# A two-layer hybrid trunk on one core: wide products in the first layer, c broadcast by DMA, and tokens sorted by t mod 4

## The chip, the core and the metric

The kernel runs on one core of a Trainium2 chip. The time is that of the device, in microseconds, for one execution of the whole program; lower is better. Several executions were timed, and one more was recorded by the hardware profiler. In the profile PE is TensorE's matmul, PEld its weight load, DVE is VectorE, ACT ScalarE, POOL GpSimd, and SP the engine whose queue issues all DMAs of this kernel.

## What is computed

One sequence of 256 tokens with 2048 features goes through two layers. Each layer is x <- LayerNorm(alpha x + (1 + gate) mixer(x (1 + scale) + shift)), where shift, scale and gate are products of silu(c) with a 2048 x 6144 matrix ("ada"), c being one vector of 2048.

- Layer A (a state-space mixer): `proj = h @ in_w`, with 4096 columns z, 4096 columns xs, 2048 columns B and C, 64 columns dt. xs, B and C go through a causal convolution of width 4 along the tokens and a silu; then a scan in one chunk of 256 tokens for 8 groups of 8 heads, a gate silu(z), an RMS norm by group, and the product with out_w (4096 x 2048).
- From the output of layer A keys and values are made for 3 groups of 8 heads of 128 (`x @ kv_w`, 2048 x 6144).
- Layer B (attention): 24 query heads in three groups (window, dilation) = (128, 1), (512, 4), (2048, 16). A query t attends t, t - d, t - 2d, ... within its window, with a linear bias in the distance. The outputs of the three groups are merged per head by their softmax denominators, which is one softmax over the keys of all three groups. Then a gate silu(z), and the product with out_w.

With 256 tokens a query of group 2 or 3 can only meet keys of the same t mod 4.

## The kernel before

Everything is in fp32 accuracy. The large products split each weight piece and each activation into a high part in the format fp32r and the low rest, and add three products: high x high, high x low, low x high. A weight piece is 128 x 1024 (512 KB), loaded by `load_piece` (L88) into one of 6 buffers, split by `split` into `whi` by ACT (L94) and `wlo` by DVE (L95), each with 4 buffers. The small products (scores, values, transposes) are in plain fp32.

There are three forms of large product:

- `tm_piece`/`tm_mults` (L172 to L174): the activations are the stationary side, the weights stream with 512 columns.
- `cm_piece` (L119 to L121), run by `cm_quad`, `cm_quads` or by hand: the weights are stationary, 256 tokens stream. For each of the 2 row tiles and 4 column blocks of a piece three matmuls of 256 columns: high x high, high x low, low x high, all into the same 128 x 256 accumulator.
- `cm_wide` (L151, L152): the high and the low half of the activations lie side by side, so one matmul with 512 columns makes high x high and high x low into the two halves of an accumulator of 128 x 512, and one of 256 adds low x high into the first half. A piece has 4 row tiles and 2 column blocks, and the two matmuls follow each other for each of them. At the end the two halves are joined: ACT copies one (L156), DVE adds the other (L157).

The order of the work:

1. *Start.* c is loaded as two rows, spread over the partitions by 8 records of matmul with a column of ones (L422), and silu'd by ACT into `cb_` (L423). Then the 32 tiles of layer A's shift and scale (1 MB each, `ada_load` L230) are multiplied with `cb_` and summed by DVE (`ada_dot` L236), and each finished pair gives one tile of h (`h_step`, L381 to L383), high and low part in `hp`. While these come in, parts of ten products are begun with the tiles of h that are there (`begun`, `order`); each part is set aside in SBUF and later added.
2. *Layer A's products* (`product`), with the scan (`stage1`, `stage2`, `stage3`) of a group beside the products of the next one. `xs` and `bc` products use `cm_quad`; the convolution `conv` reads the accumulator where it is (L302, L305), or the sum with the set-aside part (L344). The dots for the gate run in the background, one in five pieces.
3. *Layer A's output* (L172 to L174 with `ylo`); `y_tiles` (L641 to L644) transposes y two tiles of 128 at a time between the pieces.
4. *LayerNorm, keys and values.* `x_tiles` (L711 to L716) transposes the normalized rows and makes high and low part; three key products by `cm_quads`, three by `cm_wide` (`wk1`), six value products. Beside them 32 more ada tiles. GpSimd multiplies the rows by the LayerNorm's gain and adds its offset (L766, L767) for the residual of layer B.
5. *Layer B*: `queries` by `cm_wide`, `attend` for 4 heads at a time, `z_gate` by `cm_wide`, then the output product and the last LayerNorm.

The order on every engine is not that of the code: `arrange` simulates the whole program with prices for each instruction, gives each a due time, tries several rounds of list scheduling, and fixes the best order per engine, the DMA queue on SP included.

## Time and profile before

| | |
|---|---|
| runs | 1283.16, 1287.76, 1289.54 us; median 1287.76 |
| profiled execution | 1281.55 us, of which the span from first to last instruction is 1279.8 |
| granted TensorE clock | 0.993 |
| DMA | 334.82 MB, mean 262 GB/s |
| busy: PE, DVE, ACT, POOL | 1239.4, 1039.2, 696.6, 33.3 us |

The profiled execution is 1.6 us below the fastest of the three runs and 6.2 below their median. Rows of the profile read: line of the kernel, engine, operation, output<-inputs with shapes, count | busy time, mean ns of one | idle time of the engine just before, and what ended it. A timeline row is start, length, engine, line, operation, names, shapes, count of records merged. A record of a matmul lasts longer than the distance to the next one, since matmuls are pipelined.

### The profile page before, as it was taken

How to read it: one execution, taken by the hardware profiler on the slowest of the kernel's cores; microseconds unless marked ns; L12 is line 12 of the kernel's file. 1: busy time of each engine (PE TensorE's matmuls, PEld its weight loads, DVE VectorE, ACT ScalarE, POOL GpSimd, SP SyncE). 2: the span in 40 equal slices, each digit the busy share in tenths (PEclk: the TensorE clock that was granted, in tenths of full speed). 3: DMA queues.
4: the chain of work that ended last, by engine and by line, in shares of the span. 5: the costliest groups of instructions: out<-in, count | busy, mean ns of one | idle time of the engine just before them, and what ended most of it. 6: DMA issues, size and time to landing. Idle time of an engine off the chain costs nothing.

```text
span 1279.8 us, 19378 instructions
## 1 busy us (share of the span) xinstructions
PE 1239.4 (97%) x7386; PEld 1095.2 (86%) x7386; DVE 1039.2 (81%) x1457; ACT 696.6 (54%) x1027; POOL 33.3 (3%) x20
## 2 busy tenths in 40 slices
PE   6999999999999999999999899999999999999995
PEld 4978999899899999788888699888888888888884
DVE  6999978999998887978895799998745647848778
ACT  4644566868577767764333444444445645444551
POOL 0000000000000000000000135000000000000000
PEclk9999999999999999999999899999999999999998
DMA  9999967887785556578997688999866663453571
GB/s 372 422 422 422 384 216 268 314 276 247 240 300 191 173 159 203 162 258 269 400 376 218 222 315 308 396 420 395 299 191 193 211 185 115 147 183 107 155 266 66
DMA packets 80449, 334.82 MB, mean 262 GB/s; under 512 B 9090, under 2 KB 9314, under 8 KB 67684
## 3 DMA queue, kind: packets, MB, share of 16 engines
q1 hardware_dynamic: 80356, 333.58, 73.5%
q8 instruction: 58, 0.95, 0.3%
q14 instruction: 35, 0.29, 0.1%
HBM read 331.37 MB, written 2.18 MB: 261 GB/s over the span
## 4 chain that ended last, share of the span: by engine, by line
PE 78%; DMA 12%; DVE 7%; ACT 1%; issue 1%; SPq 0%; DVEq 0%; ACTq 0%
PE acc L151 12%; PE acc L174 11%; PE acc L173 11%; PE acc L172 11%; PE acc L152 6%; DMA raw<-in_win 6%; PE acc L119 6%; PE acc L121 6%; PE acc L120 6%; DMA araw<-in_ada 5%; DVE wlo L95 2%; PE py L589 1%; DVE araw L236 1%; PE aux L795 1%; PE po L819 1%
## 5 line engine op out<-in xcount | busy, mean ns | idle before, releaser
L95 DVE TENSOR_TENSOR wlo<-raw,whi 128x1024 fp32r<-128x1024 f32 x395 | 488.9, 1244 | 176.5 <-ACT whi L94 175.2
L94 ACT ACTIVATE whi<-raw 128x1024 fp32r<-128x1024 f32 x395 | 417.1, 1057 | 382.1 <-PE acc L174 178.6
L119 PE MATMUL acc<-actT,whi 128*128 128x256 f32 x960 | 273.6, 288 | 11.8 <-ACT actT L382 7.4
L173 PE MATMUL acc<-wlo,actT 128*128 128x512 f32 x704 | 276.4, 393 | 0.6 <-DVE wlo L95 0.6
L172 PE MATMUL acc<-whi,actT 128*128 128x512 f32 x704 | 274.8, 393 | 1.6 <-ACT whi L94 1.0
L121 PE MATMUL acc<-actT,wlo 128*128 128x256 f32 x960 | 270.5, 285 | 1.4 <-DVE wlo L95 1.4
L120 PE MATMUL acc<-actT,whi 128*128 128x256 f32 x960 | 271.3, 285 | 0.0
L151 PE MATMUL acc<-actT,whi 128*128 128x512 f32 x704 | 251.3, 398 | 0.0
L236 DVE SCALAR_TENSOR_TENSOR araw<-araw,cb__72 128x2048 f32<-128x2048 f32 x96 | 218.4, 2286 | 9.0 <-DMA araw<-in_ada 5.7
L152 PE MATMUL acc<-actT,wlo 128*128 128x256 f32 x704 | 201.8, 287 | 0.6 <-DVE wlo L95 0.6
L119 PEld LDWEIGHTS acc<-actT,whi 128*128 128x128 f32 x960 | 185.2, 194 | 15.7 <-ACT actT L382 9.0
L121 PEld LDWEIGHTS acc<-actT,wlo 128*128 128x128 f32 x960 | 184.0, 193 | 2.3 <-DVE wlo L95 2.0
L120 PEld LDWEIGHTS acc<-actT,whi 128*128 128x128 f32 x960 | 185.1, 193 | 0.3
L174 PE MATMUL acc<-whi,actT 128*128 128x512 f32 x448 | 175.1, 391 | 0.0
L172 PEld LDWEIGHTS acc<-whi,actT 128*128 128x128 f32 x704 | 131.9, 188 | 30.1 <-ACT whi L94 2.8
L151 PEld LDWEIGHTS acc<-actT,whi 128*128 128x128 f32 x704 | 132.2, 188 | 29.2
L173 PEld LDWEIGHTS acc<-wlo,actT 128*128 128x128 f32 x704 | 132.3, 188 | 27.5 <-DVE wlo L95 1.1
L152 PEld LDWEIGHTS acc<-actT,wlo 128*128 128x128 f32 x704 | 133.0, 189 | 1.9 <-DVE wlo L95 1.2
L174 PE MATMUL acc<-whi,ylo 128*128 128x512 f32 x256 | 100.8, 394 | 0.0
L174 PEld LDWEIGHTS acc<-whi,actT 128*128 128x128 f32 x448 | 84.1, 188 | 17.5 <-issue 0.5
L174 PEld LDWEIGHTS acc<-whi,ylo 128*128 128x128 f32 x256 | 48.1, 188 | 9.4
L305 DVE SCALAR_TENSOR_TENSOR cacc<-acc,prm,cacc 128x255 f32<-128x255 f32 (+2 forms) x96 | 43.7, 475 | 2.7 <-ACT cacc L302 2.3
(205 smaller groups left out, 1083.1 us busy)
## 6 DMA issues: line engine op xcount, KB each, us to landing
araw<-in_ada SPq DMA_DIRECT2D x96, 1024.0 KB, 7.2
raw<-in_win SPq DMA_DIRECT2D x160, 512.0 KB, 4.9
raw<-in_wkv SPq DMA_DIRECT2D x72, 512.0 KB, 4.9
raw<-in_wout SPq DMA_DIRECT2D x64, 512.0 KB, 5.6
raw<-in_wbin SPq DMA_DIRECT2D x64, 512.0 KB, 4.0
raw<-in_wk SPq DMA_DIRECT2D x24, 512.0 KB, 6.6
cbc<-cumd SPq DMA_DIRECT2D x16, 512.0 KB, 5.3
raw<-in_wbout SPq DMA_DIRECT2D x16, 512.0 KB, 4.3
```

What stands on the lines that cost most here:

```text
L94: S.activation(hi, raw, AF.Copy)
L95: V.tensor_tensor(lo, raw, hi.bitcast(F32), op=ALU.subtract)
L119: T.matmul(o, hi[:, k, c_], ahi[:, kt, :], start=first, stop=False, skip_group_check=True)
L120: T.matmul(o, hi[:, k, c_], alo[:, kt, :], start=False, stop=False, skip_group_check=True)
L121: T.matmul(o, lo[:, k, c_], ahi[:, kt, :], start=False, stop=kt == k1 - 1, skip_group_check=True)
L151: T.matmul(ps[n], hi[:, k, c_], xp[:, kt], start=kt == 0, stop=False, skip_group_check=True)
L152: T.matmul(ps[n][:, 0, :], lo[:, k, c_], xhi[:, kt, :], start=False, stop=kt == KT - 1, skip_group_check=True)
L172: T.matmul(ps[b], h_, hi[:, k, :], start=kt == k0, stop=False)
L173: T.matmul(ps[b], h_, lo[:, k, :], start=False, stop=False)
L174: T.matmul(ps[b], l_, hi[:, k, :], start=False, stop=kt == k1 - 1)
L236: V.scalar_tensor_tensor(raw, raw, 1.0, cb_, op0=ALU.mult, op1=ALU.mult, accum_out=mod[layer][:, ct, j:j + 1])
L305: V.scalar_tensor_tensor(acc[:, o:], ps[:, :L - o], w[:, j:j + 1], acc[:, o:], op0=ALU.mult, op1=ALU.add)
```

## The change

Nine edits are made together.

- `cm_wide` becomes general and takes over the `xs` and `bc` products 1 to 7 and 2, 4, 6 of layer A (`cm_quad` goes). Their weights come as a new array `wsub` in pieces of 4 row tiles x 256 columns. `hp` is laid out tile by tile with the high and low half side by side. Without a set-aside part the two halves are joined by an ACT copy and a DVE add into a new tile `ct`; with one, DVE adds both halves to it, one after the other.
- In every `cm_wide` the 8 matmuls of 512 columns of a piece come first, then the 8 of 256 columns.
- c is broadcast to all partitions by four DMAs of 512 columns, and silu'd in place; the rows and the 8 matmul records go.
- The first shift and scale tile are loaded and dotted in two halves, whose sums are added.
- `y_tiles` makes the four transposes of two tiles before their reads.
- `x_tiles` writes the tokens sorted by t mod 4, so keys, values, queries and the attention's output are in that order; the gated output is put back in order when it is split, by 8 instructions instead of 2 on each of ACT and DVE.
- In `attend` a block of 128 queries (two classes of t mod 4) takes 128 keys each for the two dilated groups, and 256 for the first: 512 scores in one PSUM tile, where it was 384 for the first block and 768 for the second. The bias of a head is made in 3 instructions, once for both blocks.
- The LayerNorm's gain and offset for the residual go from GpSimd to DVE. The bias table (768 columns of distance and 768 of mask) lies in `cb_` instead of a buffer of its own.
- The planner prices a DMA that writes to DRAM 3 us longer. The order of all engines is planned anew.

```diff
-    def cm_quad(src, ahi, alo, rate=(0, 1), k0=0):
+    def cm_wide(src, both, high, rate=(0, 1), k0=0):
         ps = acc_pair()
-        for q in range(k0 // 2, KT // 2):
-            cm_piece(src, q, ps, ahi, alo, k0=k0)
+        for q in range(k0 // 4, KT // 4):
+            hi, lo = (t.rearrange("p k n -> p (k n)").rearrange("p (k n) -> p k n", k=4)
+                      for t in split(load_piece(src[q])))
+            halves = [(k, n, slice(n * P, n * P + P)) for k in range(4) for n in range(2)]
+            for k, n, c_ in halves:
+                T.matmul(ps[n], hi[:, k, c_], both[:, 4 * q + k], start=4 * q + k == k0, stop=False, skip_group_check=True)
+            for k, n, c_ in halves:
+                T.matmul(ps[n][:, 0, :], lo[:, k, c_], high[:, 4 * q + k, :], start=False, stop=4 * q + k == KT - 1,
+                         skip_group_check=True)
             background(*rate)
         return ps
...
+        n = 2 if (layer, ct) == (0, 0) and kind != "gate" else 1
+        for i in range(n):
+            c_ = slice(D // n * i, D // n * i + D // n)
+            nc.sync.dma_start(raw[:, c_], ada[layer, KIND.index(kind), ct][:, c_])
...
-                ps = cm_quad(src, hhi, hlo, rate=R, k0=k0)
-                t = tiles(ps)
-                if part is not None:
-                    for w in range(2):
-                        V.tensor_tensor(part[:, 2 * w:2 * w + 2, :], ps[w], part[:, 2 * w:2 * w + 2, :], op=ALU.add)
-                    t = [part[:, n, :] for n in range(4)]
+                t = []
+                for w in range(2):
+                    ps = cm_wide(wsub[2 * WSUB.index((kind, g)) + w], hp, hhi, rate=R, k0=k0)
+                    for n in range(2):
+                        if part is None:
+                            t.append(p0.tile([P, L], F32, name="ct", bufs=4))
+                            S.activation(t[-1], ps[n][:, 1, :], AF.Copy)
+                            V.tensor_tensor(t[-1], ps[n][:, 0, :], t[-1], op=ALU.add)
+                        else:
+                            t.append(part[:, 2 * w + n, :])
+                            for i in range(2):
+                                V.tensor_tensor(t[-1], ps[n][:, i, :], t[-1], op=ALU.add)
...
-                for i in range(2):
-                    row = szt[i].rearrange("p b n -> p (b n)")[:1]
-                    nc.sync.dma_start(row, c[:, 1024 * i:1024 * i + 1024])
+                for i in range(4):
+                    bcast(cb_[:, 512 * i:512 * i + 512], c, 512 * i)
+                    S.activation(cb_[:, 512 * i:512 * i + 512], cb_[:, 512 * i:512 * i + 512], AF.Silu)
...
+            pt = pt.rearrange("p (j r) -> p r j", r=4)
-            S.activation(xhi[:, kt, :], pt, AF.Identity, bias=b_, scale=g_)
+            S.activation(xhi[:, kt, :].rearrange("p (r j) -> p r j", r=4), pt, AF.Identity, bias=b_, scale=g_)
...
-                PO.tensor_tensor(u[b][:, cs_], u[b][:, cs_], lnr[0], op=ALU.mult)
-                PO.tensor_tensor(u[b][:, cs_], u[b][:, cs_], lnr[1], op=ALU.add)
+                V.tensor_tensor(u[b][:, cs_], u[b][:, cs_], lnr[0], op=ALU.mult)
+                V.tensor_tensor(u[b][:, cs_], u[b][:, cs_], lnr[1], op=ALU.add)
...
+                for g in (1, 2):
+                    T.matmul(pq[:, (g - 1) * P:g * P], qq[:, g, i, cb], kk[hq][:, g, i, cb], start=True, stop=True)
+                T.matmul(pq[:, 2 * P:], qq[:, 0, i, cb], kk[hq][:, 0, i, :], start=True, stop=True)
...
+            T.matmul(po, v[:, 0, 0, ci], pT[:, :, 2, :], start=True, stop=False)
+            T.matmul(po, v[:, 0, 1, ci], pT[:, :, 3, :], start=False, stop=False)
+            for b in range(2):
+                for g in (1, 2):
+                    T.matmul(po[:, b * P:b * P + P], v[:, g, b, ci], pT[:, b, g - 1, :], start=False, stop=b == 1 and g == 2)
...
-        return 0.36, 0.0, None, _n(o) * list(o.ap)[0][1] * 4
+        return 0.36, 3.0 if str(o.bass_ap.tensor.space) == "DRAM" else 0.0, None, _n(o) * list(o.ap)[0][1] * 4
```

More of the change, by code (lines that the diff above doesn't have):

```diff
@@ L266, in drain @@
             jobs.pop(0)()
[L269 to L270 removed]
+    hp = act.tile([P, KT, 2, L], F32R, name="actT")
+    hhi, hlo = hp[:, :, 0, :], hp[:, :, 1, :]
     with ExitStack() as cA:
@@ L419, in trunk @@
                 nc.sync.dma_start(adab_, par[:, :NB])
-                for i in range(4):
-                    pc = mm.tile([P, 512], F32, name="acc")
-                    T.matmul(pc, ones[:1, :], szt[i // 2][:1, i % 2, :], start=True, stop=True)
-                    S.activation(cb_[:, 512 * i:512 * i + 512], pc, AF.Silu)
                 V.tensor_scalar(adab[:, :, :, 1:3], adab[:, :, :, 1:3], 1.0, None, op0=ALU.add)
```

134 lines of the change are left out of this document (64 added, 70 removed).

## The prediction

> **What bounds the kernel now.** I read the page from the top: the busy shares, the 40 slices, the chain. Then I cut the span into stages with the view of windows, because the shares are means over stages with different limits.
>
> ```profile
> span 1279.8 us, 19378 instructions
> PE 1239.4 (97%) x7386; PEld 1095.2 (86%) x7386; DVE 1039.2 (81%) x1457; ACT 696.6 (54%) x1027; POOL 33.3 (3%) x20
> PE 78%; DMA 12%; DVE 7%; ACT 1%; issue 1%; SPq 0%; DVEq 0%; ACTq 0%
> ```
> ```profile
> 17.00:132.00 115.00, 108.77 (x667) 96.74 (x668) 106.19 (x114) 60.39 (x81) 0.00 (x0) 1.00 1.02 422
> 150.00:540.00 390.00, 388.15 (x2695) 359.25 (x2693) 343.15 (x541) 278.57 (x461) 0.00 (x0) 1.00 0.69 231
> 728.00:812.00 84.00, 82.87 (x651) 81.23 (x652) 82.13 (x84) 39.49 (x50) 33.08 (x16) 0.98 0.87 314
> 1002.00:1222.00 220.00, 220.00 (x1291) 193.08 (x1291) 149.30 (x271) 105.19 (x171) 0.00 (x0) 1.00 0.51 156
> ```
>
> In the windows the columns are window, length, busy PE, weight loads, DVE, ACT, POOL (with counts), granted clock, DMA share, GB/s. The reader is to see four regimes. Up to about 150 us the DMA engines are full (1.02, 422 GB/s), and the chain runs through them. From 150 to 540 (the layer A products) PE is at 388 of 390, DVE at 88%. From 728 to 812 (first K product, after the LayerNorm) PE and DVE are both full. From 1002 to 1222 (queries and attention) PE is never idle and DVE has 71 us to spare. So from 150 us on a part is worth what it takes from PE's stream of matmuls, and in the first 150 us what it takes from or adds to the DMA stream.
>
> A busy PE is not a measure of its stream, since records overlap; I take distances from start to start.
>
> ```profile
> 438.11 0.28 PE L121 MATMUL acc<-actT,wlo 128*128 128x256 f32 x1
> ...
> 444.95 0.28 PE L121 MATMUL acc<-actT,wlo 128*128 128x256 f32 x1
> ```
> ```profile
> 659.64 0.39 PE L172 MATMUL acc<-whi,actT 128*128 128x512 f32 x1
> ...
> 667.80 0.39 PE L172 MATMUL acc<-whi,actT 128*128 128x512 f32 x1
> ```
> ```profile
> 1030.08 0.40 PE L151 MATMUL acc<-actT,whi 128*128 128x512 f32 x1
> ...
> 1038.92 0.40 PE L151 MATMUL acc<-actT,whi 128*128 128x512 f32 x1
> ```
> ```profile
> 31.08 0.40 PE L172 MATMUL acc<-whi,actT 128*128 128x512 f32 x1
> ...
> 32.24 0.39 PE L174 MATMUL acc<-whi,actT 128*128 128x512 f32 x1
> ```
>
> 57 steps of 256 columns in 6.84 us are 0.120 us each. 36 steps of 512 columns in 8.16 us are 0.2267. 25 pairs of 512 and 256 in turn take 8.84, 0.3536 a pair. In a busier place 5 steps of 512 take 1.16, 0.232 each.
>
> **The change, part by part.** *1. Order in the wide products.* wk1 has 6 products and wbin 16, of 4 pieces each: 88 pieces of 8 pairs. In turn a piece takes 8 x 0.3536 = 2.829. Grouped, all but one pair costs 0.2267 + 0.120 = 0.3467, a gain of 7 x 0.0069 = 0.048 a piece, 4.3 us in all. If 512 after 512 goes at 0.232 here, the pair is 0.352 and the gain 1.0; that it saves nothing is the end on that side, and it could cost if both forms went slower, which no row shows. I take -3.0, nearer to the undisturbed rows, since these stages are PE-bound with DVE at 68%. It also leaves DVE 1.8 us more for the low half of each piece; where PE never waits that is worth nothing.
>
> *2. Wide products in layer A.* Products xs 1 to 7 and bc 2, 4, 6 cover 12 + 6 x 16 + 12 + 4 + 4 = 128 tiles of the contraction, with 4 blocks each: 512 places, where three matmuls of 256 (0.360) become a pair. Grouped it is 0.3467, or 0.352 by the disturbed row: -6.8 to -4.1, I take -5.3. The bytes and splits stay (64 pieces before and after). New is the joining of the two halves of an accumulator:
>
> ```profile
> L157 DVE TENSOR_TENSOR qq<-acc,qq 128x256 f32<-128x256 f32 x32 | 13.4, 420 | 8.1 <-ACT qq L156 8.1
> L156 ACT ACTIVATE qq<-acc 128x256 f32<-128x256 f32 x32 | 12.0, 379 | 21.0 <-PE acc L152 21.0
> L344 DVE TENSOR_TENSOR y<-acc,y 128x512 f32<-128x512 f32 x8 | 5.4, 685 | 0.6 <-PE acc L121 0.6
> ```
> ```profile
> ACT whi L94 <- PE acc L174: 36.9, 26, 2.2
> DVE wlo L95 <- ACT whi L94: 36.7, 42, 2.6
> ```
>
> xs 2 to 7 have 24 tiles without an earlier part: 24 x 0.420 on DVE (10.1) and 24 x 0.379 on ACT (9.1). The four products with a part get 32 adds (13.4) for 8 wide ones (5.5). DVE goes from 343 to 361 us in a stage that shrinks to 385: 94%; ACT to 75%. In the waits of 150 to 540 (the second fence) DVE stands still for ACT, and ACT for PE to free a buffer: the splits run ahead of PE, so this is cover. It gets thin, and I charge +1.0 for short waits, with 0 and the rival below as ends. Two of the four tiles of a product now end at half time, so the convolutions come in two smaller bursts; I count nothing for that.
>
> *3. Attention.* With tokens sorted by t mod 4, groups 1 and 2 need only their own block. Per head the score matmuls were three of 128 and three of 256 columns and become four and two; the value matmuls alike; 9 transposes become 8.
>
> ```profile
> 1080.73 0.60 PE L819 MATMUL po<-pT,vt 128*128 128x256 f32 x2
> 1081.16 0.39 PE L820 MATMUL po<-pT,vt 128*128 128x128 f32 x2
> 1081.39 0.60 PE L819 MATMUL po<-pT,vt 128*128 128x256 f32 x2
> ...
> 1082.70 1.03 PE L795 MATMUL aux<-kk,qq 128*128 128x256 f32 x4
> ```
> ```profile
> 1089.84 0.60 PE L809 MATMUL po<-cc,sc 128*128 128x128 f32 x4
> 1090.20 0.36 PE L152 MATMUL acc<-actT,wlo 128*128 128x256 f32 x1
> ```
>
> A matmul of plain fp32 shows as two records (x2). One of 256 takes 0.43 (1080.73 to 1081.16) and one of 128 0.23 (to 1081.39). A head's scores fall from 1.98 to 1.78 and its values as much; a transpose is 0.36 / 4 = 0.09. That is 0.49 a head, 3.9 us for 8, and up to 1 us more because six small groups per head become larger and PE switches less: -3.9 to -5. I take -4.3. DVE and ACT get fewer and larger instructions in a stage where DVE idles 71 us: nothing. The strided reads and writes of the sort and the four-way split of the attention output are off PE's path; the end that follows 1222 I leave as it is. The bias table grows by half, at a time when DMA is at 0.51: nothing.
>
> *4. c by DMA, first ada tiles in halves.*
>
> ```profile
> 0.74 0.64 SPq L415 DMA_DIRECT2D sz<-in_c  x2
> 1.43 0.35 SPq L230 DMA_DIRECT2D araw<-in_ada  x1
> ```
> ```profile
> 9.47 0.60 ACT L423 ACTIVATE cb__72<-acc 128x512 f32<-128x512 f32 x1 [1.11 <-PE acc L422]
> 10.10 2.29 DVE L236 SCALAR_TENSOR_TENSOR araw<-araw,cb__72 128x2048 f32<-128x2048 f32 x1 [3.30 <-ACT cb__72 L423]
> 16.87 0.79 PE L119 MATMUL acc<-actT,whi 128*128 128x256 f32 x2 [7.43 <-ACT actT L382]
> ```
> ```profile
> 131.36 14.15 DMA raw<-in_win
> 145.59 1.07 ACT whi L94
> ```
>
> Two loads of 4 KB become four broadcasts of 256 KB: 1.05 MB more through a stream that is full until about 145 us, 2.5 us at 422 GB/s. They stand first in SP's queue, ahead of the ada tiles, so everything behind them on that queue lands later. The stream starts 0.7 us earlier (0.74 for 1.43). Against that the dot products start earlier: c lands near 5 us, the silus (0.60 each) follow it, and the halves of 0.52 MB land every 1.24 us, so the first matmul comes near 12.7 instead of 16.87. But the chain leaves this stage through a weight piece that DMA delivers at 145.6, and not through the first dot. So +1.8, between +2.7 (no earlier start, small packets) and -2.4 (4.2 earlier carried through). The extra halves and adds on DVE, some 0.6 us, are in that range.
>
> *5. LayerNorm gain from POOL to DVE.*
>
> ```profile
> 731.18 2.72 POOL L766 TENSOR_TENSOR u<-u,lnr 128x512 f32<-128x512 f32 x2 [730.74 <-ACT actT L714]
> 732.67 2.31 DVE L95 TENSOR_TENSOR wlo<-raw,whi 128x1024 fp32r<-128x1024 f32 x1
> 739.04 1.21 DVE L95 TENSOR_TENSOR wlo<-raw,whi 128x1024 fp32r<-128x1024 f32 x1
> ```
>
> While POOL runs, the same DVE split takes 2.31 us instead of 1.21. POOL is busy 33 us between 728 and 812, and about a dozen DVE instructions there are stretched by 1.1: 13 us. The 16 adds and multiplies cost DVE 16 x 0.685 = 11.0 (the 512-wide row of part 2), and can be done until the queries. The Trainium skill, page "SBUF — State Buffer", section "Who interferes with whom", says that a DVE instruction with two SBUF inputs contends with a GpSimd instruction that reads SBUF; by that rule the stretch goes away whole, and the trace agrees in size. PE's matmuls here are nearly dense, so only some waits of PE are to be had: -1.5, from 0 to -3.
>
> *6. Transposes of y in fours* (540 to 582): PE waited 0.5 us before them, and half the switches go: -0.5, from 0 to -1. *7. The planner's longer delay for writes to DRAM* and the new order that it makes: 0, +-4.
>
> ```profile
> L641 PE MATMUL aux<-cc,y 128*128 128x128 f32 x64 | 11.4, 273 | 0.5 <-DVE ylo L644 0.5
> ```
>
> Sum: -3.0 - 5.3 + 1.0 - 4.3 + 1.8 - 1.5 - 0.5 = -11.8. The profiled execution took 1281.55 (span 1279.8), so it would become 1269.8. The median of the three runs is 1287.76, 6.2 above it; from there it is 1276.
>
> **The rivals.** *A, the order saves little.* A 512 among others goes at the slower pace, as in the pair of 0.3536 now. Then part 1 is 0 and part 2 is 512 x (0.360 - 0.3536) = -3.3: 5.0 less gain, 1281. For it: the row at 31 us. Against: 36 steps at 0.2267. The Trainium skill, page "TensorE: Matmul & The Clock Gate", section "Back-to-back issue gap", gives N / 2.4 + 2.5 ns, the same in any order; an estimate by that page is 0 for part 1 and 512 x 2.5 ns = 1.3 us for part 2, 1283. The trace has 120 ns where the page gives 109, so the rows decide, but the rule belongs to this rival.
>
> *B, slower: DVE becomes the bound of layer A.* If 88% busy is all that DVE can reach in this pattern of dependences, its 361 us need 361 / 0.88 = 410 instead of 390: +20 where I have -4.3, 1300. It decides from the point where PE's accumulators or the four split buffers wait for DVE; with 94% needed the margin is 24 us. For it: from 728 to 812 DVE at 98% goes with short stops of PE. Against: the waits, where DVE waits 36.7 us for others.
>
> *C, the early start carries through.* PE and DVE get 4 us ahead and stay so; part 4 becomes -2.4, the whole -16: 1272. For it: PE's 6 us of idle time after 17. Against: a DMA share of 1.02.
>
> *D, the new order is a worse one.* All instructions are ordered anew; +4 to +8 by added waits of a few tenths each: 1280 to 1284. Nothing in the trace before speaks for or against.
>
> **How the numbers follow.** Forecast 0.47 (1272 to 1280), A 0.17, B 0.06, C 0.18, D 0.12. About 0.5% (6.4 us) is what a measurement of this kernel tells from no change; faster is below 1281.3. Faster: the forecast, C, over half of A, a third of D: 0.77. Same: the rest of A and D, 0.16. Slower: B and a little, 0.07. The range 1267 to 1286 leaves out B, the far end of D and a little below C.
>
> **What would show it.** Start-to-start 0.347 a pair in wide products, at 800 and at 1030; the stage of layer A's products shorter by 4; no 2.31 us splits; attention shorter by 4; the first matmul before 14 us, and the last ada tile later than before. It would be wrong if DVE in 150 to 540 shows PE waiting for wlo, or if the DMA stream ends earlier.

## The result, and the profile after

The changed kernel took 1267.94 us in the median of 4 runs (1266.99 to 1269.07). In the same comparison the kernel before took 1288.35. The ratio is 0.985, 95% interval 0.9821 to 0.9878: faster by 1.5%, some 19 us, where 1276 was forecast with a range of 1267 to 1286. The median lies 0.9 us inside the lower end of that range. The profiled execution took 1266.99, 14.6 us less than the 1281.55 of the profile before.

The page of the changed kernel: the span, the busy times, the chain by engine, and the 512-column matmuls of the wide products (before, 704 of them at L151; the others are layer A's).

```profile
span 1265.2 us, 18365 instructions
PE 1218.5 (96%) x6858; PEld 1062.8 (84%) x6858; DVE 1038.2 (82%) x1469; ACT 699.8 (55%) x1033; POOL 0.2 (0%) x4
PE 81%; DMA 9%; DVE 6%; issue 2%; ACT 1%; DVEq 0%; SPq 0%; ACTq 0%
L144 PE MATMUL acc<-actT,whi 128*128 128x512 f32 x1216 | 310.8, 395 | 0.0
```

The reader sees that PE still bounds the kernel, with 21 us less busy time; DVE's 1038 us are as before (1039): what it gets in layer A and for the LayerNorm it saves elsewhere, as the windows below show. To see where the 14.6 us lie, I cut both traces at the same four matmuls: the first with `dtrow`, the first transpose of y, the end of the first three K products, the end of the V products. First the four timeline rows that give the first two cuts (two of before, two of after).

```profile
180.83 0.33 PE L453 MATMUL acc<-cc,dtrow 64*128 64x64 f32 x2
537.44 0.39 PE L641 MATMUL aux<-cc,y 128*128 128x128 f32 x2
```
```profile
175.01 0.34 PE L462 MATMUL acc<-cc,dtrow 64*128 64x64 f32 x2
525.75 0.50 PE L649 MATMUL aux<-cc,y 128*128 128x128 f32 x3
```

Then the windows between the cuts, before and after (the first row of after is the start, to set beside the prediction's row from 17 to 132): layer A's products, the first K products, the other K and the V products, layer B to its last product. Columns as in the prediction: window, length, busy PE, PEld, DVE, ACT, POOL, clock, DMA share, GB/s.

```profile
180.80:537.40 356.60, 355.51 (x2447) 328.40 (x2447) 316.94 (x506) 260.26 (x434) 0.00 (x0) 1.00 0.68 231
726.70:803.20 76.50, 75.40 (x607) 74.59 (x608) 75.69 (x79) 36.89 (x48) 33.08 (x16) 0.97 0.86 307
803.20:1001.60 198.40, 197.80 (x964) 166.78 (x962) 151.20 (x160) 97.45 (x126) 0.00 (x0) 1.00 0.85 311
1001.60:1221.40 219.80, 219.80 (x1291) 192.92 (x1290) 149.35 (x271) 104.99 (x171) 0.00 (x0) 1.00 0.51 156
```
```profile
17.00:132.00 115.00, 111.84 (x716) 102.18 (x717) 107.16 (x114) 62.67 (x83) 0.00 (x0) 1.00 1.02 422
175.00:525.70 350.70, 349.31 (x1935) 301.13 (x1935) 330.89 (x562) 266.81 (x462) 0.00 (x0) 1.00 0.69 237
714.40:790.10 75.70, 75.16 (x608) 74.76 (x609) 70.71 (x86) 36.92 (x48) 0.00 (x0) 0.96 0.94 349
790.10:992.00 201.90, 198.91 (x963) 166.56 (x962) 152.71 (x169) 97.52 (x127) 0.00 (x0) 1.00 0.81 294
992.00:1206.50 214.50, 214.50 (x1282) 190.38 (x1281) 136.77 (x209) 101.05 (x149) 0.00 (x0) 1.00 0.48 159
```

The stages give: up to the dt row -5.8 us, layer A -5.9, first K products -0.8, the other K and V products **+3.5**, layer B -5.3, the rest (layer A's output, the end) -0.3: together -14.6. Two of these have the other sign than forecast: the start, for which +1.8 stands in the prediction, and the V stage, where the grouping should have helped. In each row the length less PE's busy time is time in which PE stood: 3.0 us of the V stage after, 0.6 before. I call the busy time the stream and the rest standing; the experiments are read by these two. The stream is only a near measure: a wait shorter than the overlap of two records stays hidden in it, and the same matmuls of the V stage have busy times from 197.70 to 200.38 us in the kernels below, against 349.10 to 349.31 in layer A and 214.40 to 214.60 in layer B.

### The profile page after: what moved, and what is told of

Same layout as the page of the kernel before. It is cut to its first block, busy times and chain, and to the rows that moved or that the text cites. A ratio compares the mean times of both kernels' runs of the same rounds, so it can differ in the third digit from the quotient of the medians.

```text
span 1265.2 us, 18365 instructions
## 1 busy us (share of the span) xinstructions
PE 1218.5 (96%) x6858; PEld 1062.8 (84%) x6858; DVE 1038.2 (82%) x1469; ACT 699.8 (55%) x1033; POOL 0.2 (0%) x4
## 4 chain that ended last, share of the span: by engine, by line
PE 81%; DMA 9%; DVE 6%; issue 2%; ACT 1%; DVEq 0%; SPq 0%; ACTq 0%
PE acc L144 20%; PE acc L172 12%; PE acc L171 12%; PE acc L170 12%; PE acc L146 10%; DMA raw<-in_win 6%; PE acc L122 3%; DMA araw<-in_ada 3%; PE acc L124 3%; PE acc L123 3%; PE py L598 2%; DVE wlo L98 2%; DVE araw L239 2%; PE po L832 1%; PE aux L808 1%
## 5 line engine op out<-in xcount | busy, mean ns | idle before, releaser
L98 DVE TENSOR_TENSOR wlo<-raw,whi 128x1024 fp32r<-128x1024 f32 x395 | 479.6, 1221 | 166.5 <-ACT whi L97 164.9
L144 PE MATMUL acc<-actT,whi 128*128 128x512 f32 x1216 | 310.8, 395 | 0.0
L144 PEld LDWEIGHTS acc<-actT,whi 128*128 128x128 f32 x1216 | 218.5, 189 | 38.4
L239 DVE SCALAR_TENSOR_TENSOR araw<-araw,cb__72 128x2048 f32<-128x2048 f32 x94 | 214.6, 2286 | 10.8 <-DMA araw<-in_ada 10.2
L146 PEld LDWEIGHTS acc<-actT,wlo 128*128 128x128 f32 x1216 | 166.0, 190 | 11.7
L172 PE MATMUL acc<-whi,actT 128*128 128x512 f32 x448 | 175.0, 391 | 0.0
L146 PE MATMUL acc<-actT,wlo 128*128 128x256 f32 x1216 | 171.1, 283 | 0.0
L122 PE MATMUL acc<-actT,whi 128*128 128x256 f32 x448 | 126.2, 290 | 19.9 <-ACT actT L395 18.4
L123 PE MATMUL acc<-actT,whi 128*128 128x256 f32 x448 | 126.8, 286 | 0.1
L124 PE MATMUL acc<-actT,wlo 128*128 128x256 f32 x448 | 125.1, 285 | 1.1 <-DVE wlo L98 1.1
L122 PEld LDWEIGHTS acc<-actT,whi 128*128 128x128 f32 x448 | 86.3, 196 | 21.2 <-ACT actT L395 18.8
L123 PEld LDWEIGHTS acc<-actT,whi 128*128 128x128 f32 x448 | 86.9, 194 | 0.6 <-DVE actT L396 0.4
L124 PEld LDWEIGHTS acc<-actT,wlo 128*128 128x128 f32 x448 | 86.0, 194 | 1.5 <-DVE wlo L98 1.5
L557 ACT ACTIVATE seg<-cbc,cumT 128x128 f32<-128x128 f32 x128 | 40.3, 389 | 9.3 <-PE py L598 6.5
```

Source lines behind the costliest of these rows:

```text
L98: V.tensor_tensor(lo, raw, hi.bitcast(F32), op=ALU.subtract)
L122: T.matmul(o, hi[:, k, c_], ahi[:, kt, :], start=first, stop=False, skip_group_check=True)
L123: T.matmul(o, hi[:, k, c_], alo[:, kt, :], start=False, stop=False, skip_group_check=True)
L124: T.matmul(o, lo[:, k, c_], ahi[:, kt, :], start=False, stop=kt == k1 - 1, skip_group_check=True)
L144: T.matmul(ps[n], hi[:, k, c_], both[:, 4 * q + k], start=4 * q + k == k0, stop=False, skip_group_check=True)
L146: T.matmul(ps[n][:, 0, :], lo[:, k, c_], high[:, 4 * q + k, :], start=False, stop=4 * q + k == KT - 1, skip_group_check=True)
```

## The experiments

The interval of a ratio is about 0.2 to 0.3% to either side, 3 to 4 us, so I read a part's worth from the distances in the trace first and from the medians second. Times in brackets are lowest and highest run. Each kernel has one profile, but for the kernel before, which has two. The recorded expectations of b_again, u_start and b_start count the start by the first matmul of the dt product (173.4 and 167.6 us), which comes some 7.4 us ahead of the row with `dtrow` used here (180.8 and 175.0); the difference of 5.8 is the same.

**The kernel before, unchanged (b_again).**

> The kernel before, unchanged, as a second look. In its first profile the execution took 1281.55 us, below all its timed runs (1283.16 to 1289.54), while the kernel after spreads over 2 us only. Theory 1 (the difference lies in the first 170 us, where PE waits for the DMA stream): the profiled span is some us longer than 1279.8, the dt rows (173.4 us in the first profile) come later by about as much, and from there to the end the distances stay within 1 us. Theory 2 (it is spread over the whole span): the dt rows come at 173 to 174 and the later stages are each a little longer.

Measured: 1285.53 (1282.17 to 1290.73), ratio 1.0006 (0.9986 to 1.0026). The profiled execution has a span of 1284.6, 4.8 more than the first. Its windows for layer A, the first K products and the V stage:

```profile
180.80:539.00 358.20, 355.74 (x2447) 328.26 (x2447) 317.08 (x506) 260.19 (x434) 0.00 (x0) 1.00 0.68 230
728.40:805.90 77.50, 76.43 (x608) 75.66 (x609) 74.87 (x79) 36.96 (x48) 32.06 (x16) 0.95 0.85 304
805.90:1006.30 200.40, 198.83 (x962) 166.85 (x962) 151.21 (x160) 97.34 (x126) 0.00 (x0) 1.00 0.84 307
```

The dt row is at the same 180.8, so the start does not vary. Of the 4.8 us, 4.6 lie in the three stages with high DVE or DMA load (+1.6, +1.0, +2.0): 5.1 us of standing for 2.8, and a busy PE that is 1 us longer in the K and in the V stage. So the first profile was a quick execution, and a stage's length can be read to about 2 us: differences of 4 us and more in a stage are read below, smaller ones only as stream. This bears on the V stage: against this second profile (200.4) the changed kernel's 201.9 is only 1.5 us longer, and the +3.5 are in part the quickness of the first.

**The start (u_start, b_start, u_whole).** In the changed kernel the old start was put back (c as two rows, broadcast by matmuls, ada tiles whole); the kernel before got the new start alone; and the changed kernel lost the halves alone.

```diff
-                for i in range(4):
-                    bcast(cb_[:, 512 * i:512 * i + 512], c, 512 * i)
-                    S.activation(cb_[...], cb_[...], AF.Silu)
+                row = szt[i]...; nc.sync.dma_start(row, c[:, ...])
+                pc = mm.tile(...); T.matmul(pc, ones[:1, :], szt[...]); S.activation(cb_[...], pc, AF.Silu)
-        n = 2 if (layer, ct) == (0, 0) and kind != "gate" else 1
+        n = 1
```

> The kernel after, with the start undone: c as two rows and the matmuls with a column of ones, the first ada tiles whole. Theory 1 (c by DMA and the halves made the first stage 5.8 us shorter, by the finer mixing of ada tiles and weight pieces that follows from them): the dt rows (167.6 us after, 173.4 before) come at 172 to 174 and the time is 1272 to 1274. Theory 2 (the finer mixing is the planner's doing for another reason, and the 1 MB of c costs what was forecast): dt rows at 165 to 167, time 1265 to 1268.

> The kernel before with the start's edit alone (c by four DMAs, first ada tiles in halves). Theory 1: dt rows at 167 to 169, time about 1281 to 1283 by the median (5 to 6 less than before). Theory 2: dt rows at 173 to 176, time within 3 us of before.

> The changed kernel, with c still by DMA but the first ada tiles whole again (no halves). All else as in the changed kernel. The start edit as a whole brought the dt row from 181 to 175 us. Theory 1: what does it is that the broadcast through TensorE and its copies are gone and the plan's order of DMAs on SP becomes finer; the halves only let the first dot begin a microsecond earlier. Then the dt row stays at 174 to 176.5 us and the time is within 2 us of the changed kernel's 1267.9. Theory 2: the halves carry it, since with whole tiles the first dot waits for 1 MB; then the dt row comes near 180 us and the time is about 1272.

Measured: the changed kernel with the old start 1272.16 (1270.24 to 1274.6), ratio 0.9892 (0.9856 to 0.9929); the kernel before with the new start 1284.37 (1280.96 to 1288.36), ratio 0.9989 (0.9972 to 1.0007); the changed kernel without halves 1267.08 (1266.91 to 1267.25), ratio 0.9835 (0.9813 to 0.9857). The dt row is at 181.2, 175.1 and 176.2 us. So the start edit is what moves it by 6 us, in either kernel, and it is c by DMA, with the plan that comes with it, that does so, not the halves: without them the dt row comes 1.2 us later and the time is the same. Windows from 17 to 132, with the old start and (kernel before) with the new one:

```profile
17.00:132.00 115.00, 108.82 (x660) 97.01 (x661) 104.81 (x114) 60.17 (x83) 0.00 (x0) 0.99 1.02 422
```
```profile
17.00:132.00 115.00, 110.67 (x710) 101.32 (x711) 107.80 (x113) 61.88 (x83) 0.00 (x0) 1.00 1.02 422
```

The DMA share and rate are the same 1.02 and 422 in all of them. With the new start PE gets 50 matmuls further in the same time. It does not begin earlier: the first matmul comes at 17.34, against 16.87 before, because ACT does two weight splits (14.46 and, not shown, 15.92) before it finishes the first tile of h:

```profile
14.46 1.06 ACT L97 ACTIVATE whi<-raw 128x1024 fp32r<-128x1024 f32 x1 [6.20 <-DMA raw<-in_win]
17.34 1.23 PE L122 MATMUL acc<-actT,whi 128*128 128x256 f32 x4 [17.34 <-ACT actT L395]
```

What differs is the order in SP's queue. With the old start it issues 3 or 4 ada tiles one after the other and then up to 6 weight pieces; with the new one, up to 105 us, 1 or 2 tiles between every 1 to 3 pieces. By 132 us the changed kernel has issued 46 weight pieces where with the old start it is 43, and its last ada tile of this stage goes out at 141.10 us and not at 130.03. PE's waits for high halves between 17 and 132 fall from 4.0 us in three waits (old start) to 1.0 in one. Behind 132 us the same windows, up to the dt row, of the kernel before and of the changed kernel:

```profile
132.00:180.83 48.83, 48.55 (x386) 47.29 (x385) 39.80 (x51) 25.46 (x35) 0.00 (x0) 1.00 0.84 296
```
```profile
132.00:175.01 43.01, 42.63 (x337) 41.37 (x335) 38.73 (x49) 22.38 (x30) 0.00 (x0) 1.00 0.92 364
```

PE is busy nearly throughout in both, with 49 matmuls fewer left in the changed kernel, and over the window the DMA engines are not full in either. By distances from start to start PE loses 0.6 us here in the kernel before and 0.7 in the changed one; between 17 and 132 us it loses 12 with the old start, in the kernel before as in the changed one, and 6 with the new. So the lead is made before 132 us, the end of this stage is PE's and not the stream's, and the 1 MB more found room there. That PE was ahead at 132 because its weight pieces came earlier is argued; no run changed the order alone. The fineness of the mixing does not decide by itself: without the halves the queue is nearly as coarse as with the old start from 47 us on (up to 3 tiles and up to 6 pieces in a row), yet 45 pieces are out by 132 us and the dt row comes at 176.2.

The lead isn't kept of itself. In the kernel before it was gone by the transposes of y (536.8 us for 537.4): layer A took 361.7 us for 356.6, and some 7 us were lost between 200 and 260, nearly all behind 225, where the unchanged kernel loses some 2 (lost: the distances from one PE start to the next above the 0.2267 and 0.120 of the two forms and the small ones' usual ones, so slow issue counts beside standing). There DVE stands with the next dot product at the head of its order, and the scan's work queues behind it:

```profile
175.10:536.80 361.70, 358.47 (x2448) 330.45 (x2448) 317.32 (x505) 259.92 (x435) 0.00 (x0) 0.99 0.67 228
```
```profile
223.04 2.29 DVE L241 SCALAR_TENSOR_TENSOR araw<-araw,cb__72 128x2048 f32<-128x2048 f32 x1 [3.77 <-DMA araw<-in_ada]
```

**Layer A's products in the old form (u_wide).** `cm_quad` again for the ten blocks, evicted from its two accumulators; the rest as in the changed kernel.

> The changed kernel, with layer A's ten blocks of products back in the form before (a 128-row weight tile against 256 columns, three matmuls, evicted from two accumulators); all else as in the changed kernel, wide products after layer A too. Theory 1 (forecast's term 2, without the grouping): the wide form saves what 512 pairs save, 512 x (0.360 - 0.352) = 4.1 us, less the price of joining halves on DVE; this kernel then takes 3 to 5 us more, 1271 to 1273, all of it in the stage from 175 to 526 us, and DVE is some 18 us less busy there. Theory 2: the gain of layer A's stage (5.9 us) came from the new order of the plan and the extra backlog of TensorE, and the wide form pays for its joins only: this kernel is within 1.5 us of the changed one.

Measured: 1274.3 (1272.98 to 1275.92), ratio 0.9911 (0.9883 to 0.994). The window of layer A:

```profile
175.50:532.30 356.80, 355.37 (x2447) 328.15 (x2447) 317.33 (x505) 257.33 (x432) 0.00 (x0) 1.00 0.66 231
```

The stream is 355.37 us, as in the kernel before (355.51), against 349.31 with the wide form: 6.1 us, which is the difference in the medians too (6.4). DVE has 13.6 us less to do here. So the first theory holds, with somewhat more than its 3 to 5 us. Rival B had its chance: DVE needed 330.89 of 350.7 us, 94% as forecast, and PE stood 1.4 us.

**512 and 256 columns in turn again (u_order).**

```diff
-            for k, n, c_ in halves:
-                T.matmul(ps[n], hi[...], both[...], ...)
-            for k, n, c_ in halves:
-                T.matmul(ps[n][:, 0, :], lo[...], high[...], ...)
+            for k, n, c_ in halves:
+                T.matmul(ps[n], hi[...], both[...], ...)
+                T.matmul(ps[n][:, 0, :], lo[...], high[...], ...)
```

> The kernel after with the wide products' matmuls in turn again (512, 256, 512, 256). In the profile after, a 512 that follows a 512 starts 0.232 later on average and a 256 after a 256 0.119, so a pair is 0.351, against 0.3536 in turn. Theory 1 (that is the gain of the order): 152 pieces x 7 pairs x 0.0025 = 2.7 us, time 1270 to 1271, attention to end unchanged in its other parts. Theory 2 (grouping also takes waits of PE for the low half away): over 4 us. Theory 3 (nothing to be measured): within 1 us of 1268.

Measured: 1266.49 (1264.31 to 1267.78), ratio 0.9852 (0.982 to 0.9883): no difference in the whole. Two pieces of the same product in the changed kernel (grouped; the counts give the matmuls of a row) and the first and last of ten pairs in turn:

```profile
1010.82 1.11 PE L146 MATMUL acc<-actT,wlo 128*128 128x256 f32 x8
1011.77 2.00 PE L144 MATMUL acc<-actT,whi 128*128 128x512 f32 x8
1013.61 0.64 PE L146 MATMUL acc<-actT,wlo 128*128 128x256 f32 x4
```
```profile
1009.79 0.40 PE L144 MATMUL acc<-actT,whi 128*128 128x512 f32 x1
...
1012.97 0.40 PE L144 MATMUL acc<-actT,whi 128*128 128x512 f32 x1
```

Grouped, 8 of 512 columns take 1.84 us (0.230 each) and 8 of 256 take 0.95 (0.119): 0.349 a pair. In turn 9 pairs take 3.18: 0.3533. So grouping does save here, 0.004 a pair where 0.0069 was the best case. The windows of the kernel in turn, for layer A, the V stage and layer B, show where it went:

```profile
174.50:524.70 350.20, 350.20 (x1936) 300.46 (x1935) 329.46 (x562) 275.11 (x468) 0.00 (x0) 1.00 0.68 237
789.00:991.20 202.20, 200.22 (x963) 166.62 (x962) 152.04 (x169) 97.19 (x125) 0.00 (x0) 1.00 0.81 291
991.20:1207.20 216.00, 216.00 (x1282) 190.32 (x1281) 138.86 (x210) 101.41 (x150) 0.00 (x0) 1.00 0.48 157
```

PE's stream is longer by 0.9, 1.3 and 1.5 us than in the changed kernel. The 1.3 of the V stage lie within the spread of its busy times; the other two, 2.4 together, lie outside theirs and are 0.002 and 0.003 for each of the 512 pairs of a stage. But PE stands 0.0 and 2.0 us in the first two where it stands 1.4 and 3.0 in the changed kernel, and the dt row comes 0.5 earlier. The shorter stream was given back by waits in the one execution that was profiled; that the other plan makes them, and not the execution, is not shown.

**The old attention (u_attn).** Tokens in their old order, old scores, bias table and split; the rest as in the changed kernel.

> The changed kernel, with the attention as before: tokens in their old order, two of three score groups over both blocks, the old bias table and four-way split undone; all else as in the changed kernel. Theory 1 (forecast's term 3): 0.49 us a head and the switches saved between the small groups, so this kernel takes 4 to 5 us more, all of it between the end of the V product and the end of the attention: about 1272.5. Theory 2: the stage before the last product is 5.3 us shorter after the change in part by the order of the matmuls in wbin and by the higher share of DVE; then this kernel takes only 2 to 3 us more, about 1270.5.

Measured: 1268.41 (1265.6 to 1271.25), ratio 0.9866 (0.9832 to 0.9899), which is hardly more than with the new attention. Layer A, the V stage and layer B:

```profile
174.10:523.20 349.10, 349.10 (x1935) 301.32 (x1935) 330.60 (x562) 265.77 (x460) 0.00 (x0) 1.00 0.70 238
787.60:985.30 197.70, 197.70 (x963) 166.99 (x962) 151.12 (x169) 97.68 (x127) 0.00 (x0) 1.00 0.82 296
985.30:1204.40 219.10, 219.01 (x1290) 193.15 (x1289) 146.71 (x270) 108.16 (x172) 0.00 (x0) 1.00 0.49 156
```

In its own stage the old attention costs 4.6 us (219.1 for 214.5), as forecast. But the V stage, with the same instructions on PE and DVE in both kernels, is 4.2 shorter, without any standing of PE (layer A, which the edit does not touch either, is 1.6 shorter, too little to be told). So the first theory holds for the stage and fails for the whole: neither expected that. What the V stage gained in length, then, does not belong to the form of its products. I put it down to the order that the planner found for one kernel and not for the other; with one profile of each, and 2.0 us between two executions of the kernel before, this is argued and not shown. What it looks like in the changed kernel (waits of PE in that stage: total, times, longest; then DVE's timeline):

```profile
PE acc L171 <- DVE wlo L98: 3.0, 3, 1.2
```
```profile
868.17 1.22 DVE L98 TENSOR_TENSOR wlo<-raw,whi 128x1024 fp32r<-128x1024 f32 x1
869.98 2.29 DVE L239 SCALAR_TENSOR_TENSOR araw<-araw,cb__72 128x2048 f32<-128x2048 f32 x1 [0.59 <-DMA araw<-in_ada]
872.20 1.22 DVE L98 TENSOR_TENSOR wlo<-raw,whi 128x1024 fp32r<-128x1024 f32 x1
```

At 870 DVE stands for an ada tile in front of a dot, then does the dot, 2.29 us, while the next low half waits behind it: 4.03 us from one split to the next (868.17 to 872.20), where a V piece takes PE 12 x 0.2267 = 2.72.

**Gain and offset on GpSimd (u_pool), and on DVE in the kernel before (b_dve).** The same two lines, put back in the one and changed alone in the other.

```diff
-                V.tensor_tensor(u[b][:, cs_], u[b][:, cs_], lnr[0], op=ALU.mult)
-                V.tensor_tensor(u[b][:, cs_], u[b][:, cs_], lnr[1], op=ALU.add)
+                PO.tensor_tensor(u[b][:, cs_], u[b][:, cs_], lnr[0], op=ALU.mult)
+                PO.tensor_tensor(u[b][:, cs_], u[b][:, cs_], lnr[1], op=ALU.add)
```

> The changed kernel, with the LayerNorm's 16 gain and offset operations back on GpSimd; all else is as in the changed kernel. The stage from the last K product to the last V product took 3.5 us more after the change (201.9 for 198.4), and the stage of the first K product only 0.9 less, although the 2.31 us splits are gone. Theory 1: the move costs more than it saves. The 16 operations sit on DVE between 873 and 895 us among the dot products, and TensorE waits there for the low halves; so with GpSimd again this kernel is 2 to 3 us faster in all: K stage 0.5 to 1.5 longer, V stage 3 to 4 shorter, about 1265.5. Theory 2: the V stage became longer by the new order of the plan, and the move saves the 1.5 us forecast: K stage 1.5 longer, V stage unchanged, about 1269.5.

> The kernel before, with one part of the change alone: the LayerNorm's 16 gain and offset operations on DVE in place of GpSimd. Taken back from the changed kernel, this part costs 8.7 us by the medians, 8.3 of them in the K stage (84.0 for 75.7 us), where DVE is then busy 83.7 us. Theory 1: the part is worth what the K stage shows in the kernel before: that stage is 76.5 us long there with GpSimd, DVE busy 75.7, with 10 dot products for 13; so it goes to 75.7 and the V stage takes what the operations bring; the time is within 2 us of the kernel before. Theory 2: the contention costs the kernel before as much as the changed one, spread over the K and V stages; then this kernel is 6 to 9 us faster, about 1279.

Measured: with GpSimd the changed kernel takes 1276.6 (1274.35 to 1278.33), ratio 0.9925 (0.9901 to 0.995); the kernel before with DVE 1283.25 (1279.86 to 1286.12), ratio 0.9978 (0.9963 to 0.9994). Both theories for the first fall: the move doesn't cost, and it saves 8 to 9 us, not 1.5. The first K products in the changed kernel with GpSimd, window and two groups of DVE:

```profile
713.70:797.70 84.00, 78.28 (x608) 76.00 (x609) 83.69 (x86) 36.87 (x48) 33.00 (x16) 0.95 0.89 320
L98 DVE TENSOR_TENSOR wlo<-raw,whi 128x1024 fp32r<-128x1024 f32 x24 | 35.0, 1469 | 0.3 <-ACT whi L97 0.3
L239 DVE SCALAR_TENSOR_TENSOR araw<-araw,cb__72 128x2048 f32<-128x2048 f32 x13 | 32.9, 2531 | 0.0
```

PE stands 5.7 us in this window (84.00 less 78.28), where in the changed kernel with DVE it stands 0.5. The largest of its waits inside the window, absent in the changed kernel, is for the low halves:

```profile
PE acc L124 <- DVE wlo L98: 3.5, 3, 2.4
```

The same groups in the changed kernel; the dots of the kernel before in this stage; and, again with GpSimd in the changed kernel, two operations of GpSimd (one record) and the dot beside them:

```profile
L98 DVE TENSOR_TENSOR wlo<-raw,whi 128x1024 fp32r<-128x1024 f32 x24 | 29.0, 1217 | 1.8 <-ACT whi L97 1.8
L239 DVE SCALAR_TENSOR_TENSOR araw<-araw,cb__72 128x2048 f32<-128x2048 f32 x13 | 29.7, 2286 | 2.2 <-DMA araw<-in_ada 2.0
```
```profile
L236 DVE SCALAR_TENSOR_TENSOR araw<-araw,cb__72 128x2048 f32<-128x2048 f32 x10 | 22.8, 2280 | 0.0
```
```profile
736.90 5.38 POOL L777 TENSOR_TENSOR u<-u,lnr 128x512 f32<-128x512 f32 x2 [12.92 <-DVE araw L239]
737.75 3.38 DVE L239 SCALAR_TENSOR_TENSOR araw<-araw,cb__72 128x2048 f32<-128x2048 f32 x1
```

The contention stretches DVE by 6.0 us in the splits, 3.2 in the dots and more in the small operations: 83.69 us for 70.71. In the changed kernel's plan 13 dots fall into this stage, and three of them meet GpSimd and take 3.38 us for 2.28; in the kernel before it is 10, none of which is stretched, and DVE's 75.69 us just fit into 76.5. (One of the ten, at 786.47, lies beside a GpSimd record that takes 7.08 us for two operations; there it is GpSimd that is long.) With the edit alone the kernel before has this K stage:

```profile
730.00:806.30 76.30, 75.77 (x607) 75.37 (x608) 69.74 (x86) 36.88 (x48) 0.00 (x0) 0.95 0.89 321
```

DVE has 6 us less to do, and the stage is as long as before: there was hardly any standing of PE to take away. The edit is worth 2.8 us there (0.9978, interval 0.8 to 4.8 us), somewhat over the 2 that the first theory allowed and below the 6 to 9 of the second; which stage it comes from, the one profile does not tell. It is a cost that comes into force when another plan fills the stage. The Trainium skill, page "SBUF — State Buffer", section "Who interferes with whom", gives the rule that such pairs lock each other out; the dots, which have two inputs in SBUF too, agree with it.

**The planner's price for a write to DRAM (u_price, b_startprice).** 0 for 3 us in the changed kernel; 3 us in the kernel before with the new start. The write is that of the scan's cumulative sums (`cumd`), which are read back, broadcast, as `cbc`.

> The changed kernel, but the planner again prices a write to DRAM at no delay; nothing else differs, only the order that the planner makes. In the kernel before, the start edit alone brought the dt row 5.7 us earlier and lost all of it again between 210 and 260 us, where the dot products wait for DMA (cumd, cbc, araw). Theory 1: what lets the changed kernel keep its early start is the 3 us price, which puts later work behind the DRAM round trip; then this kernel loses 3 to 6 us between 210 and 260 us and takes about 1272. Theory 2: layer A's wide form gives TensorE shorter streams and DVE's work other places, and the price matters little: within 1.5 us of the changed kernel, 1267 to 1269. In either case the dt row stays near 175 us.

> The kernel before, with two parts of the change: the start (c by DMA, halves) and the planner's 3 us for a write to DRAM. With the start alone the dt row came at 175.1 us, but TensorE then lost 6.5 us between 225 and 260 us, so that the y transposes came at 536.8 and the whole took 1284.4. Theory 1: the loss is made by the order of the plan around the DRAM write of the cumulative sums, and the price moves it: between 225 and 260 us 1 to 2 us are lost, the y transposes come at 531 to 533, and the time is 1279 to 1281. Theory 2: the price is worth nothing here either (without it the changed kernel was faster by 3 to 5 us), and the loss has to do with GpSimd or DVE's load: the y transposes stay within 2 us of 536.8, and the time within 3 us of 1284.

Measured: the changed kernel without the price 1263.09 (1261.87 to 1264.3), ratio 0.9824 (0.9794 to 0.9855): faster rather than slower, and the intervals overlap. The kernel before with start and price 1283.18 (1279.69 to 1285.37), ratio 0.9961 (0.9938 to 0.9984), transposes of y at 536.5. My idea that the price keeps the early start falls twice. In the kernel before, layer A takes 360.9 us with the price and 361.7 without it, where it was 356.6: some 6 us are lost between 200 and 260 with the price, 7 without it and 2 in the unchanged kernel, and the rest behind 260. In the changed kernel without the price PE never stands in layer A, and the V stage is as long as with it; the span's 3.4 us are spread (1.0 up to the dt row, 1.5 in layer A, 0.9 behind layer B), each too little to be told by itself:

```profile
174.00:523.20 349.20, 349.20 (x1935) 301.33 (x1935) 330.05 (x562) 265.64 (x460) 0.00 (x0) 1.00 0.68 238
787.70:989.60 201.90, 199.09 (x964) 166.67 (x963) 151.58 (x170) 97.88 (x127) 0.00 (x0) 1.00 0.81 295
```

**Without the price, and gain and offset behind the first queries (u_late).** In 256-column pieces, from the buffers of layer B, so that DVE does them where it has time.

> The changed kernel with two edits: a write to DRAM priced at no delay again (by itself 1263.1), and the LayerNorm's gain and offset operations in 256-column pieces behind the first queries, in the stage where DVE stands still most, so that none is left in the K and V stages. All else as in the changed kernel. With the price edit alone the stage from the K product's end to the V product's end is 201.9 us, with 3.5 us of it lost between 847 and 867, where DVE does low halves, dot products and a bunch of those operations. Theory 1: the bunch makes the loss; then this stage takes 198 to 199 us, the stages behind stay as they are, and the time is 1259 to 1261. Theory 2: the loss comes from the dot products that wait for ada tiles at the change from wide products to V products; then the stage keeps 201 to 202 us and the time is 1262.5 to 1265, with DVE busier behind 990 us.

Measured: 1262.09 (1259.93 to 1266.59), ratio 0.9801 (0.9771 to 0.9831), span 1260.4. V stage and layer B:

```profile
788.40:988.10 199.70, 198.27 (x963) 166.93 (x962) 143.56 (x154) 97.32 (x126) 0.00 (x0) 1.00 0.80 293
988.10:1202.60 214.50, 214.50 (x1283) 190.40 (x1282) 147.10 (x242) 101.50 (x149) 0.00 (x0) 1.00 0.51 168
```

The V stage falls by 2.2 us, to 199.7: between the two theories. DVE has 8 us less to do there and 10 more in layer B, at no cost. 1.4 us of standing remain, where DVE has dots that wait for ada tiles ahead of low halves. This is the fastest version run, some 5 us below the changed kernel by the spans (1260.4 for 1265.2) and the medians (1262.09 for 1267.94); by the ratios, 0.9801 for 0.985, the intervals just touch. That it beats the version with the price edit alone can't be told. Two edits were not taken back alone: the transposes of y in fours, and the place of the bias table.

## Why the prediction was right, and where it was not

The time fell into the range, by 0.9 us at its lower end; the sign and the mechanism of the three terms of PE's stream were right. The sum of -11.8 was too small: profile to profile it is -14.6, and from median to median (1286.09 for the kernel before over 19 runs, 1267.94) it is -18.2. By stages two errors of opposite sign stand out. The start was forecast at +1.8 and came to -5.8, 7.6 better; the V stage should have gained some 0.8 (the wk1 part of the order term) and lost 3.5, 4.3 worse. The other stages lie within 1.6 us of their terms. Without the V stage's loss (3.5 us against the first profile, 1.5 against the second of the kernel before) the time would lie below the range; that it lies inside is luck.

- *The profile's place among the runs.* I added 6.2 us for the distance of the first profile to a median of three. The profile before was indeed quick, 4.5 below the median of 19 runs, and the one after is 0.9 below its own. What the quick execution lacked is standing in the stages with high DVE load (5.1 for 2.8 us), so the terms worked out from it may have missed waits that the change could take away; that it took just these away is not shown.
- *1, order: mechanism right, size too large, worth nothing in the whole.* The stream gained 0.9 us in layer A, where the forecast had 2.0, and 1.5 in layer B, where its share was 2.2; what the V stage gained can't be told. The 512 among others goes at 0.230, between my rows of 0.2267 and 0.232. That a stream of PE that bounds the stage hands every saved microsecond to the end was the weak step: in the kernel in turn the longer stream goes with less standing, and the time is the same.
- *2, wide layer A: right.* 6.1 us of stream for 5.3, and 1.4 of standing for the 1.0 charged. Rival B didn't come: DVE attained 94% of the stage, and PE never waited there for a low half.
- *3, attention: right in its stage* (4.6 for 4.3).
- *4, start: wrong sign.* The failed step is "the chain leaves this stage through a weight piece that DMA delivers at 145.6, and not through the first dot", from which I priced bytes at their rate. The chain named the last wait, but from 132 us to the dt row PE was busy 48.55 of 48.83 us in the kernel before, with the DMA engines at 0.84: this end had room for 1 MB more. The last ada tile was issued later, as forecast (141.10 for 130.11), and still the dt row came 5.8 earlier, with PE 49 matmuls ahead at 132 us. That the weight pieces' coming earlier put it ahead is argued. Rival C, the early start carried through, had the outcome (-5.8 for its -2.4) by another way: the first matmul came at 17.34 us, not before 14, because ACT was at weight splits.
- *5, LayerNorm: mis-sized in the changed kernel.* -1.5, from 0 to -3, fits the kernel before (2.8); in the changed one it is 8 to 9, because I took the cover of the old plan for granted.
- *6, transposes of y: can't be told.* The stretch from them to the first K products is 0.6 us shorter (188.7 for 189.3), where -0.5 was forecast; that is too little to be read.
- *7, planner's order: 0, +-4 was fair, in each stage.* The V stage became 3.5 longer (1.5 against the second profile of the kernel before), and the kernels with the same V instructions took from 197.7 (old attention) over 201.9 to 204.7 (old start, last row below), one execution each.

```profile
794.90:999.60 204.70, 200.38 (x963) 167.87 (x962) 151.27 (x169) 97.55 (x127) 0.00 (x0) 0.99 0.80 288
```

Taken out one by one by their spans, the parts are worth: start 7.6 us, LayerNorm 8.9, wide form 5.8, order 0.8, attention -1.4, price -3.4: 18.3 together for 14.6 measured. By the medians they are 4.2, 8.7, 6.4, -1.5, 0.5 and -4.9: 13.4 together. The two ways differ by 5 us, so the sum can't be read closer than that; and each part takes a new plan with it, so the parts need not add.

## What to carry to other kernels

Where a list scheduler orders all engines anew, separate an edit's stream (busy time of the bounding engine in the stage) from its waits: the first came out within about 1 us a stage from start-to-start distances here, while stages that an edit does not touch differed by up to 7 us (197.7 to 204.7), of which 2 were seen between two executions of one kernel. Price contention by how full the victim is in the new plan, not in the old one. And a full DMA stream isn't priced by bytes alone; look at what the bounding engine is waiting for in it, and whether the stage's end is still bound by the stream.

## What was not expected of the hardware

Contention with GpSimd stretches not only the 1.21 us splits but also the dot products: 3.38 us for 2.28, the same 1.1 us for an instruction twice as long. In the changed kernel a 512-column matmul right behind another one takes 0.231 us from start to start (median) in the wide products of layer A, of the V stage and of layer B, against 0.2267 in the value products of the same V stage, so the pace goes with the kind of product and not with the stage; why is open. In the first K stage, two executions of the same kernel had a granted clock of 0.97 and 0.95 and a busy PE of 75.40 and 76.43 us; the changed kernel had 0.96 and 75.16, so the clock does not order them.
